# One decoder layer on one core: the first four products run as a group, x turned by VectorE and DRAM past 512 columns, and dense scores as three fp32r products

## The chip, the cores and the metric

The kernel runs on one core of one Trainium2 chip. The metric is the device time of one execution in microseconds (us). The kernel before takes 2049.03 us, the median of three runs that lie between 2048.91 and 2049.04.

## What is computed

One layer over 256 tokens of width 2048 in float32: a SwiGLU half, a mixer, a second SwiGLU half, each with an RMS norm ahead of it and a residual, and a last norm.

```python
def swiglu(x, w_gate, w_up, w_down):
    return (jax.nn.silu(x @ w_gate) * (x @ w_up)) @ w_down
...
    x = x + 0.5 * swiglu(rmsnorm(x, ffn1_norm[i]), ffn1_w_gate[i], ffn1_w_up[i], ffn1_w_down[i])
    x = x + hybrid_mixer(rmsnorm(x, mix_norm[i]), w_in[i], ..., w_att_out[i], w_sg_out[i], w_out[i])
    x = x + 0.5 * swiglu(rmsnorm(x, ffn2_norm[i]), ffn2_w_gate[i], ffn2_w_up[i], ffn2_w_down[i])
return rmsnorm(x, final_norm)
```

The mixer projects the normed x by one matrix into queries, keys, values and the two gating branches. Attention has 12 heads of width 128 in three groups of four: the first group looks back 128 tokens (dense), the second takes every 4th token, the third every 16th.

## The kernel before

**Products.** All weights, 1552 tiles of 128 rows by 512 columns, are read once. A weight tile is split into two fp32r halves: ScalarE copies it to `wh` (L139) and VectorE writes the rest, tile minus `wh`, to `wl` (L140). The activations are split likewise into `hi` and `lo` and stand transposed, with 128 features on the partitions and the 256 tokens along a row. A product with a weight tile is then six matmuls (L149): for each of the two halves of the tokens `hh`, `hl` and `lh`, which are hi by `wh`, hi by `wl` and lo by `wh`. Each has the activations as stationary operand and 512 weight columns as moving operand.

**Steps and units.** A step (one entry of `hus`) is two weight tiles, so 12 matmuls; there are 776 steps. A unit is two steps, 1 MB, and is one load (`load_unit`, L121). The raw buffers hold three units, `wh` and `wl` four steps each (`LA + 1`). After the products of step i the loop issues what is due there (`callbacks`) and then splits step i + 4 (`advance`). The order of a matrix's units is laid out by `lay_out`: one gate, up or down matrix slice of 512 columns after the other, and in a pair the last unit of both comes at the end.

**x at the start.** The first norm's gain is folded into x as it is transposed: TensorE transposes 128 by 128 blocks of x into PSUM (`first_transposes`, L235, two blocks for each k of the 16), ScalarE writes `xhi` (L239) and VectorE `xlo` (L240). These transposes stand between the products of the first six steps (`begin`, `early`, `midway`). The other gains are transposed by one more TensorE instruction (`gains`, L761).

**Turns.** Everywhere else a block of 256 tokens by 512 features is transposed by `turn`: VectorE transposes blocks of 32 by 32 (L191), SP writes the block to DRAM (L175) and three steps later reads it back with the partitions exchanged, in four transfers (L181); after that it is split into hi and lo (L163, L164), for x with the gain first (L264).

**Order of work.** Every engine runs its own list in the order in which the program issues it. All loads, turns and writes stand in SP's one queue.

**Scores.** For each of the four head slots and the two parities of the query, the scores of the dense group are one fp32 matmul with 256 keys (L560), read in token order from keys that are stored by parity, and those of the other groups one fp32 matmul each with 128 keys (L562). A turned q or k is copied by parity, one half by ScalarE (L513), one by VectorE (L514).

Of the kernel before, what the change touches and what calls it, by code (L numbers as in the profile page):

```python
# [41 lines left out]
def layer(ctx: ExitStack, tc: tile.TileContext, a, out):  # L42
# [24 lines left out]

    rows = sb.tile([60, P], F32, name="rows")

# [4 lines left out]

    load_rows(0, ACT)
    half = sb.tile([P, 2], F32, name="half")
    DVE.memset(half, -0.5)
    pad = big.tile([P, 96], F32, name="pad")
    DVE.memset(pad[:, 0:2], 0.0)
    junk = sb.tile([P, NC], BF16, name="junk")  # L80
    DVE.memset(junk, 0.0)
    ident = sb.tile([P, P], F32, name="ident")
# [10 lines left out]
    ss = {}  # L93
    gcols = sb.tile([P, 60], F32, name="gcols")

# [23 lines left out]
    raws, splits = {}, {}  # L119

    def load_unit(i, parts=(0, 4)):  # L121
        g, u, _ = hus[2 * i]
        if i in raws:
            r = raws[i]
        else:
            r = raws[i] = big.tile([P, UK, NC], F32, tag="raw", bufs=RAWB, name=f"raw{i}")
        k0 = g["rows0"] + u * UK * P
        src = g["w"][k0:k0 + UK * P, g["c0"]:g["c0"] + NC].rearrange("(k p) c -> p k c", p=P)
        k = slice(*parts)
        SP.dma_start(r[:, k], src[:, k])  # L130

# [110 lines left out]
    def residual(e, n, c, banks, scale, norm):  # L242
# [29 lines left out]
    def ffn(wg, wu, wd, down_post, pair):  # L272
        halves = ((0, 6), (6, 11))
        for hf, (f0, f1) in enumerate(halves):
# [8 lines left out]
            for f in range(f0, f1):  # L283
# [29 lines left out]

                gemm(wg, f * NC, 0, KD, lhs_x, post_gate, pair and f == 0)
                gemm(wu, f * NC, 0, KD, lhs_x, post_up)
            for c in range(4):
                gemm(wd, c * NC, f0 * NC, 4 * (f1 - f0), lhs_h,
                     lambda e, banks, c=c, hf=hf: down_post(e, c, banks, hf == 1), c == 0)

# [3 lines left out]

    ffn(a["ffn1_w_gate"][0], a["ffn1_w_up"][0], a["ffn1_w_down"][0], down1, False)

# [156 lines left out]
    def post_qk(key, gi):  # L482
        def post(e, banks):
            q = sb.tile([P, NT, NSLOT, HD], F32, tag="tmp", bufs=2, name=f"{key}{gi}")

            if "q" not in mix:
                qkT = big.tile([P, 2, NGRP, 2, NSLOT, P], F32, tag="A", name="qkT")
                mix["q"], mix["k"] = qkT[:, 0], qkT[:, 1]
            dst = mix[key][:, gi].rearrange("p r h (t i c) -> p r (h t) i c", t=NT, i=4)

# [58 lines left out]
    def attention(e):  # L549
        for s in range(NSLOT):  # L550
# [5 lines left out]
            def qk(s=s, got=got):  # L556
                got["b"] = [tp_bank(f"sc{s}_{r}") for r in range(2)]
                for r, b in enumerate(got["b"]):
                    q, k = mix["q"][:, :, r, s], mix["k"]
                    PE.matmul(b[:, 0:S], q[:, 0], k[:, 0, :, s].rearrange("p r c -> p c r"), start=True, stop=True)  # L560
                    for g in (1, 2):
                        PE.matmul(b[:, (g + 1) * P:(g + 2) * P], q[:, g], k[:, g, r, s], start=True, stop=True)  # L562

# [86 lines left out]
    for j in range(3):  # L650
        gemm(w_in, o_s + j * NC, 0, KD, lhs_x, post_gelu("vs", j), j == 0)
    for j in range(3):
# [11 lines left out]
    for c in range(4):  # L664
        gemm(a["w_out"][0], c * NC, 0, KD, lambda: (mix["mhi"], mix["mlo"]),
             lambda e, banks, c=c: residual(e, 2, c, banks, 1.0, True), c == 0)

# [87 lines left out]
    norm_open(0)  # L755
    first_banks[1] = mm_bank("xt1")
    first_banks[2] = mm_bank("xt2")

    def gains():
        b = tp_bank("gc1")  # L760
        PE.transpose(b[:, 0:60], rows, ident[0:60, 0:60])  # L761
        DVE.tensor_copy(gcols[:, 16:60], b[:, 16:60])

    at(20, lambda: [load_rows(i) for i in range(1, 4)])
    at(60, gains)
# [15 lines left out]

    def ready(i, whole=False):
        ks = (2 * i, 2 * i + 1)
        for k in ks:
            first_transposes(k)
        for j, k in enumerate(ks):
            first_evac(k)
            if not whole:
                split(i, slice(j, j + 1))
        if whole:  # L790
            split(i)

    def begin():
        split(0, slice(0, 1))
        for k in (0, 1):
            first_transposes(k)
            first_evac(k)
        split(0, slice(1, 2))
        products(0, jjs=(0,))
        for t in range(NT):  # L800
            product(0, 1, t, "hh")
        for k in (2, 3):
            first_transposes(k)
            first_evac(k)
        for kind in ("lh", "hl"):
            for t in range(NT):
                product(0, 1, t, kind)
        for k in (0, 1):
            split(1, slice(k, k + 1))

    begin()
    early = {2: (3, False), 3: (4, True), 5: (7, True)}
    midway = {1: (2, False), 3: (5, True), 4: (6, True)}
    for i in range(n):
        if i in early:
            ready(*early[i])
        if 0 < i < n - LA - 1:
            if i in midway:
                products(i, jjs=(0,), high_first=i < 3)
                ready(*midway[i])  # L820
                products(i, jjs=(1,), high_first=i < 3)
            else:
                products(i, high_first=i < 3)
# [58 lines left out]
```

## Time and profile before

| | |
|---|---|
| median of 3 runs | 2049.03 us |
| the profiled execution, device time | 2049.03 us |
| its span | 2047.3 us |
| TensorE matmuls (PE) busy | 2037.1 us, 100% |
| VectorE (DVE) busy | 1181.6 us, 58% |
| ScalarE (ACT) busy | 973.9 us, 48% |
| moved by DMA | 469.35 MB, mean 229 GB/s |

The span is the time from the first to the last recorded instruction; 1.73 us of the device time lie outside it. PE is the matmul stream and PEld the loading of the stationary operand, which runs beside it. SPq is SP's queue of transfers. The duration of one matmul in the profile includes its way through the array; what it takes of the stream is the distance to the start of the next one.

### The profile page before, as it was taken

What the parts mean: (1) busy time and instruction counts of PE and PEld (TensorE: products, weight loads), DVE (VectorE), ACT (ScalarE), POOL (GpSimd) and SP (SyncE); (2) the same over time, 40 slices, a digit from 0 to 9 for tenths busy, and PEclk for the clock granted to TensorE, in tenths of its full rate; (3) what the DMA queues carried; (4) which work ended last, traced back from release to release, by engine and by line L of the source; (5) the groups of instructions that cost most, each with busy time, mean ns of one, the idle gap of its engine ahead of it and who ended that gap; (6) DMA issues with size and microseconds to landing.
All of it is one profiled execution on the core that took longest, in us unless ns stands there. A gap on an engine that the chain in (4) does not pass through costs nothing.

```text
span 2047.3 us, 23805 instructions
## 1 busy us (share of the span) xinstructions
PE 2037.1 (100%) x9486; PEld 1781.6 (87%) x9486; DVE 1181.6 (58%) x1192; ACT 973.9 (48%) x1070; POOL 12.4 (1%) x18
## 2 busy tenths in 40 slices
PE   9999999999999999999999999999999999999998
PEld 7888888888888888888888888888888888888887
DVE  5555555555556557665665555565555555555554
ACT  6444444444445555455554444564444444444443
POOL 0000000000000000000000000000000000000000
PEclk9999999999999999999999999999999999999999
DMA  7777876666776866787866666777777666777764
GB/s 271 234 236 226 272 245 216 201 222 224 243 229 220 269 201 201 238 280 257 262 212 224 225 225 207 245 250 235 220 243 226 226 205 205 221 222 242 232 214 144
DMA packets 246775, 469.35 MB, mean 229 GB/s; under 512 B 11084, under 2 KB 38536, under 8 KB 246536
## 3 DMA queue, kind: packets, MB, share of 16 engines
q1 hardware_dynamic: 246344, 467.30, 70.4%
q8 instruction: 74, 1.21, 0.2%
q10 hardware_dynamic: 320, 0.53, 0.1%
q14 instruction: 37, 0.30, 0.0%
HBM read 439.22 MB, written 28.57 MB: 228 GB/s over the span
## 4 chain that ended last, share of the span: by engine, by line
PE 99%; issue 0%; ACT 0%; DVE 0%; POOLq 0%; POOL 0%
PE mm L149 98%; PE sc L560 0%; PE sp L458 0%; PE warm L748 0%; PE pv L600 0%; PE sc L562 0%; PE xt L235 0%; PE pv L596 0%; ACT x L716 0%; ACT xhi L239 0%; PE pv L597 0%; DVE x L701 0%; POOLq L877 0%; POOL rf L708 0%; ACT wh L139 0%
## 5 line engine op out<-in xcount | busy, mean ns | idle before, releaser
L140 DVE TENSOR_TENSOR wl<-raw,wh 128x1024 fp32r<-128x1024 f32 (+1 forms) x780 | 948.1, 1218 | 822.1 <-ACT wh L139 818.0
L139 ACT ACTIVATE wh<-raw 128x1024 fp32r<-128x1024 f32 (+1 forms) x780 | 818.0, 1052 | 1007.6 <-PE mm L149 974.6
L149 PE MATMUL mm<-wh,xhi 128*128 128x512 f32 x2144 | 813.8, 380 | 0.5 <-ACT wh L139 0.4
L149 PE MATMUL mm<-wh,xlo 128*128 128x512 f32 x2144 | 812.5, 379 | 0.0
L149 PE MATMUL mm<-wl,xhi 128*128 128x512 f32 x2144 | 811.8, 379 | 0.0
L149 PEld LDWEIGHTS mm<-wh,xhi 128*128 128x128 f32 x2144 | 405.3, 189 | 58.5 <-ACT wh L139 0.8
L149 PEld LDWEIGHTS mm<-wl,xhi 128*128 128x128 f32 x2144 | 405.4, 189 | 57.2
L149 PEld LDWEIGHTS mm<-wh,xlo 128*128 128x128 f32 x2144 | 405.1, 189 | 57.3
L149 PE MATMUL mm<-wh,hhi 128*128 128x512 f32 x704 | 266.8, 379 | 0.0
L149 PE MATMUL mm<-wl,hhi 128*128 128x512 f32 x704 | 266.8, 379 | 0.0
L149 PE MATMUL mm<-wh,hlo 128*128 128x512 f32 x704 | 266.8, 379 | 0.0
L149 PEld LDWEIGHTS mm<-wh,hhi 128*128 128x128 f32 x704 | 133.1, 189 | 18.9
L149 PEld LDWEIGHTS mm<-wl,hhi 128*128 128x128 f32 x704 | 133.1, 189 | 18.9
L149 PEld LDWEIGHTS mm<-wh,hlo 128*128 128x128 f32 x704 | 133.1, 189 | 18.9
L149 PE MATMUL mm<-wh,uT 128*128 128x512 f32 x192 | 58.0, 379 | 0.0
L149 PE MATMUL mm<-wh,mhi 128*128 128x512 f32 x128 | 48.5, 379 | 0.0
L149 PE MATMUL mm<-wl,mhi 128*128 128x512 f32 x128 | 48.5, 379 | 0.0
L149 PE MATMUL mm<-wh,mlo 128*128 128x512 f32 x128 | 48.5, 379 | 0.0
L149 PEld LDWEIGHTS mm<-wh,uT 128*128 128x128 f32 x192 | 36.3, 189 | 5.1
L149 PE MATMUL mm<-wl,uT 128*128 128x512 f32 x96 | 36.4, 379 | 0.0
L304 DVE SCALAR_TENSOR_TENSOR sg<-mm,rstd,sg 128x512 f32<-128x512 f32 x44 | 30.9, 744 | 0.0
L219 ACT ACTIVATE junk<-x 128x512 bf16<-128x512 f32 x30 | 18.9, 629 | 25.0 <-DVE x L247 18.6
(142 smaller groups left out, 596.9 us busy)
## 6 DMA issues: line engine op xcount, KB each, us to landing
raw<-in_w_in_dram SPq DMA_DIRECT2D x92, 1024.0 KB, 5.1
raw<-in_ffn_w_up_dram SPq DMA_DIRECT2D x88, 1024.0 KB, 5.2
raw<-in_ffn_w_down_dram SPq DMA_DIRECT2D x88, 1024.0 KB, 5.1
raw<-in_ffn_w_gate_dram SPq DMA_DIRECT2D x84, 1024.0 KB, 5.1
raw<-in_w_out_dram SPq DMA_DIRECT2D x16, 1024.0 KB, 5.0
raw<-in_w_sg_out_dram SPq DMA_DIRECT2D x12, 1024.0 KB, 5.8
bmh<-bth SPq DMA_DIRECT2D x22, 512.0 KB, 2.9
sg<-bmh SPq DMA_DIRECT2D x88, 128.0 KB, 5.0
```

Source lines behind the costliest of these rows:

```text
L139: ACT.activation(wh[:, k], r[:, k], AF.Copy)
L140: DVE.tensor_tensor(wl[:, k], r[:, k], wh[:, k].bitcast(F32), op=OP.subtract)
L149: PE.matmul(g["ps"][t], act[:, k, t * P:(t + 1) * P], in_turn(w[:, jj]), start=k == 0 and kind == "hh", stop=k == g["nk"] - 1 and kind == ...
L219: ACT.activation(junk, x[:, t, c * NC:(c + 1) * NC], AF.Square, accum_out=ss[n][:, t, c:c + 1])
L304: DVE.scalar_tensor_tensor(two(sg[:, t]), banks[t], rstd[:, t:t + 1], two(sg[:, t]), op0=OP.mult, op1=OP.mult)
```

## The change

- **Group.** The gate and up products of the first two slices form a group of four (`FIRST`). The bounds 1, 2 and 4 make it run the first step (two k) of all four, then the second of all four, then the third and fourth of all four, then steps five to eight of one after the other. Eight PSUM banks collect them: the second slice takes banks of the other tag. A unit of the group can hold steps of two matrices and is then two loads of 512 KB.
- **x.** Only k = 0 to 3 (512 columns) are transposed by TensorE. The other three blocks of 512 columns go through `turn_x`, the same way that later x blocks take: issued at steps 0, 7 and 8, read back at 1, 10 and 11, scaled and split at 4, 12 and 13. x is loaded in this order: columns 0 to 255, 512 to 1023, 256 to 511, and the last two blocks at steps 3 and 4.
- **Gains.** They are transposed by VectorE and DRAM (at steps 32, 36 and 40) instead of TensorE.
- **Scores.** The turned q and k of the dense group are split into hi and lo, k in token order, and the score is three fp32r matmuls with 256 keys. The tiles of q, k, v and the probabilities get other places in memory.
- The memset of `junk` comes first.

```diff
-    def gemm(w, c0, rows0, nk, lhs, post, pair=False):
-        gemms.append(dict(w=w, c0=c0, rows0=rows0, nk=nk, lhs=lhs, post=post, pair=pair))
+    def gemm(w, c0, rows0, nk, lhs, post, group=(1, ()), bank=None):
+        gemms.append(dict(w=w, c0=c0, rows0=rows0, nk=nk, lhs=lhs, post=post, group=group, bank=bank or mm_bank))
...
-            gs = gemms[i:i + 2] if gemms[i]["pair"] else gemms[i:i + 1]
-            i += len(gs)
-            units = [(g, u) for g in gs for u in range(g["nk"] // UK)]
-            if len(gs) == 2:
-                units.sort(key=lambda q: q[1] == q[0]["nk"] // UK - 1)
-            for g, u in units:
-                hus.extend([(g, u, 0), (g, u, 1)])
+            size, bounds = gemms[i]["group"]
+            steps = [(g, q) for g in gemms[i:i + size] for q in range(g["nk"] // 2)]
+            i += size
+            steps.sort(key=lambda s: sum(s[1] >= (b if b > 0 else s[0]["nk"] // 2 + b) for b in bounds))
+            hus.extend((g, q // 2, q % 2) for g, q in steps)
+    PAIR = (2, (-2,))
+    FIRST = (4, (1, 2, 4))
...
+        (g, u, j), (h, v, _) = hus[2 * i], hus[2 * i + 1]
+        first, last = parts
+        while first < last:
+            end = last if (g, u) == (h, v) or first > 1 else min(last, 2)
+            q, w, k = (g, u, 0) if first < 2 else (h, v, 2)
+            o = 2 * hus[2 * i + k // 2][2] - k if (g, u) != (h, v) else 0
+            k0 = q["rows0"] + w * UK * P
+            src = q["w"][k0:k0 + UK * P, q["c0"]:q["c0"] + NC].rearrange("(k p) c -> p k c", p=P)
+            SP.dma_start(raws[i][:, first:end], src[:, first + o:end + o])
+            first = end
...
-            g["ps"] = [mm_bank(f"mm{i}_{q}") for q in range(NT)]
+            g["ps"] = [g["bank"](f"mm{i}_{q}") for q in range(NT)]
...
-    def turn(i, name, q, put, dst, ev, lag=8):
+    def turn(i, name, q, put, dst, ev, lag=8, read=3):
...
-        at(i + 3, back)
+        at(i + read, back)
...
+        turn_x(e + (6 if c == 1 else 2), n, c, 6)
+    def turn_x(i, n, c, lag, read=3):
         def evac(src):
             for j in range(4):
                 v = src[:, 2 * j:2 * j + 2]
             ks = slice(4 * c, 4 * c + 4)
             split_psum(turned(xT["hi"][:, ks]), turned(xT["lo"][:, ks]), src)
 
-        turn(e + (6 if c == 1 else 2), f"x{n}_{c}", 8, put_tokens(lambda: x[:, :, cs]),
-             lambda: flat(sb.tile([P, NT, NC], F32, tag="gate", bufs=2, name=f"xt{n}_{c}")), evac, 6)
+        turn(i, f"x{n}_{c}", 8, put_tokens(lambda: x[:, :, c * NC:(c + 1) * NC]),
+             lambda: flat(sb.tile([P, NT, NC], F32, tag="gate", bufs=2, name=f"xt{n}_{c}")), evac, lag, read)
...
+                bank = tp_bank if group is FIRST and f == 1 else mm_bank
+                gemm(wg, f * NC, 0, KD, lhs_x, post_gate, group if f == 0 else (1, ()), bank)
+                gemm(wu, f * NC, 0, KD, lhs_x, post_up, bank=bank)
...
+                if gi > 0:
+                    dst = by_parity(mix[key, gi])
+                    ACT.activation(dst[:, 0], v[:, 0], AF.Copy)
+                    DVE.tensor_copy(dst[:, 1], v[:, 1])
+                elif key == "q":
+                    hi, lo = (by_parity(p) for p in mix["q", 0])
+                    for r in range(2):
+                        split_psum(hi[:, r], lo[:, r], v[:, r])
+                else:
+                    split_psum(*(p.rearrange("p (m i b) -> p m i b", i=4, b=32) for p in mix["k", 0]), src)
...
-                    PE.matmul(b[:, 0:S], q[:, 0], k[:, 0, :, s].rearrange("p r c -> p c r"), start=True, stop=True)
+                    q0 = [p[:, (4 * r + s) * P:(4 * r + s + 1) * P] for p in mix["q", 0]]
+                    k0 = [p[:, s * S:(s + 1) * S] for p in mix["k", 0]]
+                    for i, j in ((0, 0), (0, 1), (1, 0)):
+                        PE.matmul(b[:, 0:S], q0[i], k0[j], start=i + j == 0, stop=i == 1)
...
-    load_unit(0, (1, 2))
+    for i, k in ((0, 1), (0, 2), (0, 3), (1, 0), (1, 1)):
+        load_unit(i, (k, k + 1))
+    load_x(NC, 2 * NC)
+    for k in (2, 3):
+        load_unit(1, (k, k + 1))
     load_x(S, NC)
-    load_unit(0, (2, 3))
-    load_unit(0, (3, 4))
-    for c in range(1, 4):
-        load_x(c * NC, (c + 1) * NC)
-        load_unit(c, (0, 2))
-        load_unit(c, (2, 4))
+    load_unit(2)
...
+    for i, fn in ((32, more_rows), (36, rows_out), (40, rows_back)):
...
+    for c, i, lag, read in ((1, 0, 4, 1), (2, 7, 5, 3), (3, 8, 5, 3)):
+        turn_x(i, 0, c, lag, read)
+    for c in (2, 3):
+        at(c + 1, lambda c=c: load_x(c * NC, (c + 1) * NC))
...
+    split(0, slice(0, 1))
+    first_x((0, 1))
+    for i, k in ((0, 1), (1, 0), (1, 1), (2, 0), (2, 1)):
+        split(i, slice(k, k + 1))
+        if i < n - LA - 1:
+            products(i, jjs=(0,), high_first=i < 4)
+            if i == 2:
+                first_x((2, 3))
+            products(i, jjs=(1,), high_first=i < 4)
+        if i != 1:
+            advance(i + LA + (2 if i else 1))
```

Places where the order changes. **ScalarE at the start**, before: `xt0` to `xt3` are transposed x, `wh0` and `wh1` the first two steps' weights.

```order
L139 ACTIVATE wh0_123<-raw0_87 128x512
L239 ACTIVATE xhi0_118<-xt0_127,gcols_84 128x256
L239 ACTIVATE xhi0_118<-xt1_121,gcols_84 128x256
L139 ACTIVATE wh0_123<-raw0_87 128x512
L239 ACTIVATE xhi0_118<-xt2_122,gcols_84 128x256
L239 ACTIVATE xhi0_118<-xt3_152,gcols_84 128x256
L139 ACTIVATE wh1_161<-raw0_87 128x512 x2
L239 ACTIVATE xhi0_118<-xt4_173,gcols_84 128x256
L139 ACTIVATE wh2_181<-raw1_95 128x512
```

and now:

```order
L145 ACTIVATE wh0_118<-raw0_87 128x512
L245 ACTIVATE xhi0_115<-xt0_122,gcols_84 128x256
L245 ACTIVATE xhi0_115<-xt1_125,gcols_84 128x256
L145 ACTIVATE wh0_118<-raw0_87 128x512
L145 ACTIVATE wh1_134<-raw0_87 128x512 x2
L145 ACTIVATE wh2_140<-raw1_93 128x512 x2
L145 ACTIVATE wh3_168<-raw1_93 128x1024
L245 ACTIVATE xhi0_115<-xt2_199,gcols_84 128x256
L245 ACTIVATE xhi0_115<-xt3_202,gcols_84 128x256
L145 ACTIVATE wh4_217<-raw2_100 128x1024
```

The evacuations of the third and fourth transposed blocks stood ahead of the weights of step 1, and stand now behind those of step 3.

**SP's queue**, before, for the loads of steps 8 to 25 (`raw4` to `raw12`):

```order
L130 DMA raw4_315<-in_ffn1_w_up_dram 128x4x512
L130 DMA raw5_317<-in_ffn1_w_up_dram 128x4x512
L130 DMA raw6_319<-in_ffn1_w_up_dram 128x4x512
L130 DMA raw7_341<-in_ffn1_w_up_dram 128x4x512
L130 DMA raw8_380<-in_ffn1_w_gate_dram 128x4x512
L130 DMA raw9_418<-in_ffn1_w_gate_dram 128x4x512
L130 DMA raw10_459<-in_ffn1_w_gate_dram 128x4x512
L130 DMA raw11_495<-in_ffn1_w_gate_dram 128x4x512
L130 DMA raw12_535<-in_ffn1_w_up_dram 128x4x512
```

and now, for steps 12 to 21: `bmx0_2` and `bmx0_3` are the writes of the third and fourth block of x, `xt0_2` and `xt0_3` their reads.

```order
L135 DMA raw6_269<-in_ffn1_w_gate_dram 128x4x512
L135 DMA raw7_303<-in_ffn1_w_up_dram 128x4x512
L181 DMA bmx0_2_324<-btx0_2_321 128x1024
L181 DMA bmx0_3_347<-btx0_3_344 128x1024
L135 DMA raw8_349<-in_ffn1_w_gate_dram 128x4x512
L187 DMA xt0_2_387<-bmx0_2_324 32x4x256 x4
L135 DMA raw9_392<-in_ffn1_w_gate_dram 128x4x512
L187 DMA xt0_3_412<-bmx0_3_347 32x4x256 x4
L135 DMA raw10_444<-in_ffn1_w_up_dram 128x4x512
```

Loads alone before; now two writes and eight reads of x stand between the loads, and the last four behind the load of steps 18 and 19.

**ScalarE at steps 12 to 17**, before:

```order
L139 ACTIVATE wh12_382<-raw6_319 128x1024
L219 ACTIVATE junk_74,ss0_120<-x_81 128x512 x2
L139 ACTIVATE wh13_400<-raw6_319 128x1024
L219 ACTIVATE junk_74,ss0_120<-x_81 128x512 x2
L139 ACTIVATE wh14_420<-raw7_341 128x1024
L219 ACTIVATE junk_74,ss0_120<-x_81 128x512 x2
L139 ACTIVATE wh15_438<-raw7_341 128x1024
L139 ACTIVATE wh16_461<-raw8_380 128x1024
L290 ACTIVATE sg7_359<-mm0_0_138,rstd0_457 128x512
L290 ACTIVATE sg7_359<-mm0_1_139,rstd0_457 128x512
L139 ACTIVATE wh17_479<-raw8_380 128x1024
```

and now:

```order
L145 ACTIVATE wh14_394<-raw7_303 128x1024
L225 ACTIVATE junk_70,ss0_117<-x_81 128x512 x2
L145 ACTIVATE wh15_417<-raw7_303 128x1024
L273 ACTIVATE xt0_2_387<-xt0_2_387,gcols_84 128x2x4x32 x4
L169 ACTIVATE xhi0_115<-xt0_2_387 128x1024
L145 ACTIVATE wh16_446<-raw8_349 128x1024
L273 ACTIVATE xt0_3_412<-xt0_3_412,gcols_84 128x2x4x32 x4
L169 ACTIVATE xhi0_115<-xt0_3_412 128x1024
L145 ACTIVATE wh17_468<-raw8_349 128x1024
L145 ACTIVATE wh18_486<-raw9_392 128x1024
L145 ACTIVATE wh19_502<-raw9_392 128x1024
```

The scaling and splitting of the third block now stands ahead of the weights of step 16, that of the fourth ahead of those of step 17.

## Rows read from the trace of the kernel before

**Rows 1.** The page: busy time of the engines, and one group's weight loads.
```profile
PE 2037.1 (100%) x9486; PEld 1781.6 (87%) x9486; DVE 1181.6 (58%) x1192; ACT 973.9 (48%) x1070; POOL 12.4 (1%) x18
...
L149 PEld LDWEIGHTS mm<-wh,xhi 128*128 128x128 f32 x2144 | 405.3, 189 | 58.5 <-ACT wh L139 0.8
```
**Rows 2.** PE's waits over the span: who, for whom, us, times, longest.
```profile
PE warm L748 <- DVE junk L81: 1.3, 1, 1.3
PE mm L149 <- ACT wh L139: 0.4, 1, 0.4
```
**Rows 3.** The chain in order of time: start us, us, what.
```profile
6.23 2.19 PE mm L149 x8
...
11.65 0.44 PE xt L235 x4
...
22.91 0.44 PE xt L235 x4
23.35 145.04 PE mm L149 x672
168.39 0.20 PE gc L761
...
824.06 2.12 PE sp L458 x18
...
988.88 0.54 PE sc L560 x2
```
**Rows 4.** Stretches: us, busy (count) of PE, PEld, DVE, ACT, POOL, PEclk, DMA, GB/s.
```profile
0.00:5.00 5.00, 3.68 (x9) 1.31 (x10) 0.63 (x5) 2.12 (x3) 0.70 (x6) 1.00 0.55 147
5.00:10.00 5.00, 4.59 (x21) 3.47 (x20) 2.93 (x6) 2.74 (x7) 0.00 (x0) 1.00 0.95 338
10.00:15.00 5.00, 4.91 (x27) 4.34 (x28) 3.91 (x9) 3.65 (x10) 0.00 (x0) 1.00 1.05 399
```
**Rows 5.** Transfers issued in the window 4.9 to 5.3 us: count, KB, us to landing.
```profile
raw<-in_ffn_w_gate_dram SPq DMA_DIRECT2D x1, 512.0 KB, 8.1
```
**Rows 6.** Turns' transfers: count, KB each, median us from issue to landing.
```profile
sg<-bmh SPq DMA_DIRECT2D x88, 128.0 KB, 5.0
...
uroom<-bmu SPq DMA_DIRECT2D x12, 128.0 KB, 7.5
bmq<-btq SPq DMA_DIRECT2D x3, 512.0 KB, 3.1
q<-bmq SPq DMA_DIRECT2D x12, 128.0 KB, 8.5
```
**Rows 7.** Timeline of SP: start, us, queue, line, transfer, count.
```profile
61.36 1.75 SPq L181 DMA_DIRECT2D sg<-bmh  x4
...
860.80 4.67 SPq L181 DMA_DIRECT2D q<-bmq  x4
```
**Rows 8.** A stretch in which four reads of a turn land behind a load.
```profile
64.00:66.00 2.00, 2.00 (x11) 1.76 (x10) 0.64 (x2) 1.06 (x1) 0.00 (x0) 1.00 1.09 257
```
**Rows 9.** Timeline of ACT: start, us, line, operation, count, idle before it.
```profile
51.88 1.06 ACT L139 ACTIVATE wh<-raw 128x1024 fp32r<-128x1024 f32 x1 [1.53 <-PE mm L149]
...
656.71 1.69 ACT L264 ACTIVATE xt<-xt,gcols 128x256 f32<-128x256 f32 x4
658.43 1.06 ACT L163 ACTIVATE xhi<-xt 128x1024 fp32r<-128x1024 f32 x1
...
864.78 2.00 ACT L139 ACTIVATE wh<-raw 128x1024 fp32r<-128x1024 f32 x2 [3.37 <-DMA raw<-in_w_in_dram]
```
**Rows 10.** Timeline of DVE, the same columns.
```profile
52.97 1.23 DVE L140 TENSOR_TENSOR wl<-raw,wh 128x1024 fp32r<-128x1024 f32 x1 [1.36 <-ACT wh L139]
...
876.02 0.44 DVE L514 COPY qkT<-q 128x512 f32<-128x512 f32 x1
876.38 1.29 DVE L191 STREAM_TRANSPOSE btk<-k 128x512 f32<-128x512 f32 x2
877.61 3.45 DVE L140 TENSOR_TENSOR wl<-raw,wh 128x1024 fp32r<-128x1024 f32 x3
```

More of the change, by code (lines that the diff above doesn't have):

```diff
@@ L65, in two @@
         return ap.rearrange("p (a c) -> p a c", a=2)
-    rows = sb.tile([60, P], F32, name="rows")
+    rows = sb.tile([64, P], F32, name="rows")
     def load_rows(i, queue=SP):
@@ L75, in layer @@
     load_rows(0, ACT)
+    junk = sb.tile([P, NC], BF16, name="junk")
+    DVE.memset(junk, 0.0)
     half = sb.tile([P, 2], F32, name="half")
@@ L79, in layer @@
     DVE.memset(pad[:, 0:2], 0.0)
-    junk = sb.tile([P, NC], BF16, name="junk")
-    DVE.memset(junk, 0.0)
     ident = sb.tile([P, P], F32, name="ident")
@@ L93, in layer @@
     ss = {}
[L94 removed]
+    gcols = sb.tile([P, 64], F32, name="gcols")
     gemms = []
@@ L121, in load_unit @@
     def load_unit(i, parts=(0, 4)):
[L122 to L130, printed above, removed]
+        if i not in raws:
+            raws[i] = big.tile([P, UK, NC], F32, tag="raw", bufs=RAWB, name=f"raw{i}")
+        (g, u, j), (h, v, _) = hus[2 * i], hus[2 * i + 1]
[8 more added lines that the diff above has]
+            first = end
     def split(i, k=slice(0, 2)):
@@ L266, in evac, with ffn @@
             split_psum(turned(xT["hi"][:, ks]), turned(xT["lo"][:, ks]), src)
-        turn(e + (6 if c == 1 else 2), f"x{n}_{c}", 8, put_tokens(lambda: x[:, :, cs]),
-             lambda: flat(sb.tile([P, NT, NC], F32, tag="gate", bufs=2, name=f"xt{n}_{c}")), evac, 6)
-    def ffn(wg, wu, wd, down_post, pair):
+        turn(i, f"x{n}_{c}", 8, put_tokens(lambda: x[:, :, c * NC:(c + 1) * NC]),
+             lambda: flat(sb.tile([P, NT, NC], F32, tag="gate", bufs=2, name=f"xt{n}_{c}")), evac, lag, read)
+    def ffn(wg, wu, wd, down_post, group):
         halves = ((0, 6), (6, 11))
@@ L312, in post_up @@
                     turn(e + 2, f"h{e}", 8, put_tokens(lambda: sg), lambda: flat(sg), ev)
-                gemm(wg, f * NC, 0, KD, lhs_x, post_gate, pair and f == 0)
-                gemm(wu, f * NC, 0, KD, lhs_x, post_up)
+                bank = tp_bank if group is FIRST and f == 1 else mm_bank
+                gemm(wg, f * NC, 0, KD, lhs_x, post_gate, group if f == 0 else (1, ()), bank)
+                gemm(wu, f * NC, 0, KD, lhs_x, post_up, bank=bank)
             for c in range(4):
                 gemm(wd, c * NC, f0 * NC, 4 * (f1 - f0), lhs_h,
-                     lambda e, banks, c=c, hf=hf: down_post(e, c, banks, hf == 1), c == 0)
+                     lambda e, banks, c=c, hf=hf: down_post(e, c, banks, hf == 1), PAIR if c == 0 else (1, ()))
     def down1(e, c, banks, last):
         residual(e, 1, c, banks, 0.5, last)
-    ffn(a["ffn1_w_gate"][0], a["ffn1_w_up"][0], a["ffn1_w_down"][0], down1, False)
+    ffn(a["ffn1_w_gate"][0], a["ffn1_w_up"][0], a["ffn1_w_down"][0], down1, FIRST)
     w_in = a["w_in"][0]
@@ L484, in post, with head, by_parity @@
             q = sb.tile([P, NT, NSLOT, HD], F32, tag="tmp", bufs=2, name=f"{key}{gi}")
[L486 to L489, printed above, removed]
+            one = 2 * NSLOT * P
+            if (key, gi) == ("q", 0):
+                parts = big.tile([P, 4, one], F32R, tag="A", name="qk0")
+                mix["q", 0], mix["k", 0] = (parts[:, 0], parts[:, 1]), (parts[:, 2], parts[:, 3])
+            elif (key, gi) == ("q", 1):
+                mix["C"] = big.tile([P, 4, one], F32, tag="C", name="vq")
+                mix["L"] = sb.tile([P, 3, one], F32, tag="L", name="pTk")
+                mix["q", 1], mix["k", 1] = mix["C"][:, 3], mix["L"][:, 2]
+                mix["q", 2] = sb.tile([P, one], F32, tag="W", name="q2")
+                mix["k", 2] = big.tile([P, one], F32, name="k2")
+            def head(nm, g, r, h):
+                return mix[nm, g][:, (4 * r + h) * P:(4 * r + h + 1) * P]
+            mix["head"] = head
+            def by_parity(v):
+                return v.rearrange("p (r m i c) -> p r m i c", r=2, i=4, c=16)
             def rows_of(v):
@@ L558, in qk @@
                 for r, b in enumerate(got["b"]):
-                    q, k = mix["q"][:, :, r, s], mix["k"]
-                    PE.matmul(b[:, 0:S], q[:, 0], k[:, 0, :, s].rearrange("p r c -> p c r"), start=True, stop=True)
+                    q0 = [p[:, (4 * r + s) * P:(4 * r + s + 1) * P] for p in mix["q", 0]]
+                    k0 = [p[:, s * S:(s + 1) * S] for p in mix["k", 0]]
+                    for i, j in ((0, 0), (0, 1), (1, 0)):
+                        PE.matmul(b[:, 0:S], q0[i], k0[j], start=i + j == 0, stop=i == 1)
                     for g in (1, 2):
-                        PE.matmul(b[:, (g + 1) * P:(g + 2) * P], q[:, g], k[:, g, r, s], start=True, stop=True)
+                        PE.matmul(b[:, (g + 1) * P:(g + 2) * P], mix["head"]("q", g, r, s), mix["head"]("k", g, r, s),
+                                  start=True, stop=True)
             def softmax(s=s, got=got):
@@ L650, in layer @@
     for j in range(3):
-        gemm(w_in, o_s + j * NC, 0, KD, lhs_x, post_gelu("vs", j), j == 0)
+        gemm(w_in, o_s + j * NC, 0, KD, lhs_x, post_gelu("vs", j), PAIR if j == 0 else (1, ()))
     for j in range(3):
@@ L665, in layer @@
         gemm(a["w_out"][0], c * NC, 0, KD, lambda: (mix["mhi"], mix["mlo"]),
-             lambda e, banks, c=c: residual(e, 2, c, banks, 1.0, True), c == 0)
+             lambda e, banks, c=c: residual(e, 2, c, banks, 1.0, True), PAIR if c == 0 else (1, ()))
     fin = {}
@@ L755, in layer, with more_rows, rows_out, rows_back @@
     norm_open(0)
[L756 to L765, printed above, removed]
+    def more_rows():
+        POOL.memset(rows[32:64], 0.0)
+        for i in range(1, 4):
+            load_rows(i)
+    def rows_out():
+        d = sb.tile([64, P], F32, name="gd")
+        DVE.transpose(d.rearrange("p (j b) -> p j b", b=32), rows.rearrange("p (j b) -> p j b", b=32))
+        xT["gains"] = m = dram.tile([64, P], F32, name="gm")
+        SP.dma_start(m, d)
+    def rows_back():
+        m = xT["gains"].rearrange("(i a) (j b) -> j a i b", a=32, b=32)
+        for j in range(4):
+            SP.dma_start(gcols[32 * j:32 * j + 32].rearrange("p (i b) -> p i b", i=2), m[j])
+    for i, fn in ((32, more_rows), (36, rows_out), (40, rows_back)):
+        at(i, fn)
     for c in range(4):
@@ L768, in layer @@
     at(12, lambda: norm_rstd(0))
-    loaded, done = 4, 8
+    loaded, done = 3, 3
     def advance(to):
@@ L779, in advance, with first_x @@
             done += 1
-    def ready(i, whole=False):
-        ks = (2 * i, 2 * i + 1)
+    for c, i, lag, read in ((1, 0, 4, 1), (2, 7, 5, 3), (3, 8, 5, 3)):
+        turn_x(i, 0, c, lag, read)
+    for c in (2, 3):
+        at(c + 1, lambda c=c: load_x(c * NC, (c + 1) * NC))
+    def first_x(ks):
         for k in ks:
             first_transposes(k)
-        for j, k in enumerate(ks):
+        for k in ks:
             first_evac(k)
[L788 to L813, printed above, removed]
-    for i in range(n):
[L815 to L823, printed above, removed]
+    split(0, slice(0, 1))
+    first_x((0, 1))
+    for i, k in ((0, 1), (1, 0), (1, 1), (2, 0), (2, 1)):
+        split(i, slice(k, k + 1))
+    for i in range(n):
+        if i < n - LA - 1:
[3 more added lines that the diff above has]
+            products(i, jjs=(1,), high_first=i < 4)
         for f in callbacks.pop(i, []):
             f()
-        if i > 4:
-            advance(i + LA + 2)
+        if i != 1:
+            advance(i + LA + (2 if i else 1))
     for t in range(NT):
```

12 lines of the change are left out of this document (4 added, 8 removed).

## The prediction

> **What bounds the kernel now.** Read first the busy times: PE, the matmul stream, is busy for the whole span, DVE and ACT for about half of it [rows 1]. Then PE's waits: two in all, 1.3 us before the first warm-up matmul and 0.4 us for a weight half at the start [rows 2]. So nothing late bounds the kernel; its own list of matmuls does, at the full granted clock (1.00, the 2.4 GHz level, in the stretches shown [rows 4]). What shortens that list shortens the time, one for one, until something that hides beside it becomes late. The chain in order of time gives the prices: 672 products in 145.04 us, 0.2158 us each, so a step of 12 takes 2.59 us [rows 3].
>
> How much cover is there? In the steady state ACT starts a step's `wh` when PE frees its buffer (idle 1.53 us before, released by PE), and `wl` is done 2.3 us later (51.88 to 54.20) [rows 9, 10]. Its products come three steps, 7.8 us, after the start. A weight half therefore waits 5.5 us for PE. At the very start this lead does not exist yet.
>
> **What the change takes out of PE's list.**
> - Transposes of x: 32 before, 8 left. Six groups of four at 0.44 us, the first and the last of them in [rows 3], are 2.64 us.
> - The transpose of the other gains: 0.20 us [rows 3]. Its way over DVE and SP, eight small transfers around steps 32 to 40, stands beside loads with 5.5 us of lead: nothing. If that lead were gone, a load would be late by their issue, about eight times 0.44 us (a quarter of 1.75 us [rows 7]).
> - Dense scores: eight pairs of fp32 passes at 0.54 us, 4.32 us, become 24 fp32r products with 256 columns. The spatial products have that type and size: 18 in 2.12 us, 0.118 us each [rows 3]. 24 of them are 2.83 us, so 1.49 us go. Bounds: half of a 512-column product, 0.108 us, gives 1.73 us; if each had to wait out its weight load of 0.189 us [rows 1], 4.54 us, a loss of 0.22 us. I take the spatial row, the nearest.
> - Gaps at the start. From 6.23 to 23.35 us are 17.12 us, 60 products (12.95) and 28 transposes at 0.11 (3.08), so 1.09 us are gaps [rows 3]. 0.46 us lie in the first eight products (2.19 us for 8 x 0.2158) and stay, since the first evacuation is the same. The other 0.63 us go: in ACT's list the weights of step 1 stood behind two more evacuations, and now follow step 0's at once.
> In sum 2.64 + 0.20 + 1.49 + 0.63 = 4.96 us.
>
> **What it adds.**
> - The second quarter-block of x (columns 256 to 511) is needed in the middle of step 2, at 6.23 + 0.46 + 30 x 0.2158 = 13.2 us. The same 3 MB are ahead of or in it as were ahead of or in the second half of unit 1 before, which landed at about 4.9 + 8.1 = 13.0 us [rows 5]. Between 0 and 0.6 us (one more 256 KB at 0.4 MB per us [rows 4]); I take 0.2.
> - The split of q and k of the dense group: DVE's copy of 0.44 us becomes two subtractions, together about one split of 1.23 us; 0.8 us more where DVE runs without a gap, and ACT stood idle for 3.37 us behind late loads shortly before [rows 9, 10]. The lead is thin there but not used up: 0, at most 0.8.
> - `junk` first, new places of tiles, two loads for one: no instruction on PE's path, taken as 0.
> - **The turned blocks of x**, the term that decides. Their reads have ACT and DVE waiting in line, and the weights of steps 16 and 17 stand behind them there. Follow the last block. PE comes to step 17 at 6.23 + 0.46 + 0.44 + 0.2 + 17 x 2.59 = 51.4 us.
>  The load of steps 10 and 11 has 8.4 MB up to its end (six units, 1 MB of x, a write, a read). 2.4 MB have moved by 10 us, then 0.40 MB per us [rows 4]: 25.0 us. The read goes at half that rate (257 GB/s at a full DMA share with reads in it [rows 8]), 1.3 us more, and the landing lags by about 1.3 us (an estimate: 3.1 MB had moved at 11.7 us and landed at 13.0): 27.6. Split of step 10: 30.0. DVE then turns block 2, splits step 11, turns block 3: 1.29 + 1.15 + 1.29 [rows 10], 33.7. The write takes 3.1 [rows 6]: 36.8. In the queue follow the load of steps 16 and 17, the four reads of block 2, the load of 18 and 19 and the four reads of block 3: 2.6 us each, 10.4 from about 35.4, plus a tail, 48 to 50 us. A second way to it: the reads of block 3 can be issued from 38 to about 41.5 us, since four took SP 4.67 us in the crowded place and 1.75 in a free one [rows 7], and reads behind a load landed 8.5 us after issue [rows 6]. I take 49.7 for the last.
>  Then ACT scales and copies for 2.65 us (52.4) [rows 9] and only then makes `wh` of step 17 (53.4); DVE subtracts block 3 (53.6) and makes `wl` (54.9). The second product of step 17, due at 51.6, waits for that: 3.3 us, some of it taken already at step 16 by block 2. After it the reads are over and the lead builds up.
>  Bounds: none, if the last reads land 5.0 us after issue, the median of a free turn [rows 6]: 46.3, `wl` at 51.5. From above 10.0 us, this and two loads late by 3.37 us each [rows 9].
> - Block 1, by the same count, is read by about 22.5 us and its step 8 has its `wl` at 27.7, due 28.3: no wait, 0.6 us in hand.
>
> The profiled execution's span is 2047.3 us, with 1.73 us around it: 2049.03, which is the median itself. 2047.3 - 4.96 + 0.2 + 3.3 = 2045.8, and with 1.73 **2047.6 us**.
>
> **A rule against the change.** The transposes cost 0.11 us each on an engine that is never idle [rows 1, 3]. The Trainium skill, VectorE: DVE Perf Modes, Rules for kernel authors, gives a 128 by 128 transpose to TensorE where PSUM will do as the target. By it the 24 should have stayed: 2.64 us of matmul time would be back and the 3.3 us wait gone, 0.7 us better than my sum. For the first block, which has time, the trace speaks the other way.
>
> **The rivals.**
> - *The reads land in time*, as in the free turn. For it: the mean traffic, 15 MB in 50 us, is under the 0.40 MB per us that were moved. Against it: the eight reads stand behind one another and two loads, as those of u and q did (7.5 and 8.5 us [rows 6]). Time: 2047.6 - 3.3 = 2044.3. The Trainium skill, DMA: Bandwidth & Descriptors, Anatomy of one DMA, gives a fixed 2.0 us plus the bytes at 436 GB/s, for the GpSimd path; an estimate by it is 2.3 us for a read of 128 KB, on the side of this rival. The rows show 5.0 to 8.5 us for these reads, so the trace does not agree.
> - *Weights late as well* (the slower side). The place is steps 18 to 21: SP issues their loads behind the reads, and the lead that hid this at 864.78 us, where ACT stood idle for a load for 3.37 us, has not been built up. If both loads are late by that, 6.7 us more: 2054.3. It decides from the point where those loads land 5 us after the last read. Against it: they are issued when step 13's buffer is free, some 10 us ahead.
> - *The scores gain nothing*, each product waiting out its weight load: 1.71 us more, 2049.3. Against it: the spatial products do not.
>
> **How the numbers follow.** My forecast 0.72, reads in time 0.15, weights late 0.05, scores 0.05, something else 0.03. A measurement of this kernel tells about 0.2%, 4.1 us, from no change, so faster is below 2044.9 us: the first rival, save its upper edge, 0.13. Slower is above 2053.1: 0.05. Within: 0.82. The likeliest case's own range is 2045.5 to 2049 (2 us less or 1.4 more wait). For 8 in 10 the range goes from 2044.6, towards the first rival, to 2049.4, the third.
>
> **What would show it.** Right: 8 transposes left at 0.11 us; sums of 0.35 us for three score products; PE without a gap over 0.6 us until 45 us; then two or three waits, together near 3 us, at 48 to 56 us, for ACT's `wh` and DVE's `wl`, with ACT just before them idle for a read of x; none later. Wrong: no such wait (then 2044.3), a wait at step 8, waits for loads after 56 us, or a granted clock below 1.00 behind the wait.

## The result: slower by 0.27%, and the profile after

| | before | after |
|---|---|---|
| median us of ten executions each | 2048.94 | 2055.43 |
| from to | 2048.47 to 2049.06 | 2048.32 to 2057.51 |
| profiled execution, span | 2047.3 | 2054.2 |

The ratio over all executions is 1.0027, 95% interval 1.0018 to 1.0035; the two medians lie 6.49 us, 0.32%, apart. The forecast was 2047.6 with an upper end of 2049.4. The changed kernel also varies by 9 us from one execution to the next, where the kernel before varies by 0.6; one of its ten, 2048.32, lies inside the forecast's range. The profiled execution took 2055.92 us, close to the median.

PE's waits after (columns as in [rows 2]):

```profile
PE mm L155 <- ACT wh L145: 3.1, 2, 2.3
PE mm L155 <- DVE wl L146: 2.6, 3, 1.0
PE warm L781 <- DVE pad L81: 1.3, 1, 1.3
PE mm L155 <- ACT xhi L245: 0.2, 1, 0.2
PE xt L241 <- DMA x<-in_x_dram: 0.2, 1, 0.2
```

These are waits for weight halves, as forecast, and more of them than forecast. The chain in order of time tells what was behind them, and where the rest of the time went (start us, us, what):

```profile
32.27 7.09 DMA bmx<-btx
39.38 6.52 DMA xt<-bmx
45.92 8.45 DMA xt<-bmx
...
54.47 1.72 ACT xt L273 x4
56.21 1.07 ACT xhi L169
...
58.44 1.23 DVE wl L146
59.72 770.97 PE mm L155 x3563
830.68 2.13 PE sp L468 x18
...
884.58 1.33 DVE qk L170 x2
...
997.10 0.36 PE sc L595 x3
```

Read it against [rows 3], at points with the same products behind them:

- Up to the first spatial products: 830.68 against 824.06, 6.62 us later. The transposes of x and of the gains (2.64 + 0.20) are gone from that stretch, so 9.46 us of new time stand in it (6.62 + 2.84).
- From there to the first score: 166.42 us against 164.82 (988.88 - 824.06), 1.60 us more. The chain runs through the split of q there (`qk`, L170, at 884.58).
- From the first score to the end of the span: 1057.1 us against 1058.4, 1.3 us less. Three score products take 0.36 us, two passes took 0.54: eight times 0.18 is 1.44 us.

The sum, 6.62 + 1.60 - 1.3, is the 6.9 us between the spans.

Nearly all of the 9.46 us stands at one place. PE's timeline (start us, us, engine, line, operation, idle before it):

```profile
48.97 0.38 PE L155 MATMUL mm<-wh,xlo 128*128 128x512 f32 x1
51.66 0.48 PE L155 MATMUL mm<-wh,xhi 128*128 128x512 f32 x1 [2.32 <-ACT wh L145]
53.11 0.48 PE L155 MATMUL mm<-wl,xhi 128*128 128x512 f32 x1 [0.96 <-DVE wl L146]
...
58.27 0.48 PE L155 MATMUL mm<-wh,xhi 128*128 128x512 f32 x1 [0.83 <-ACT wh L145]
59.72 0.48 PE L155 MATMUL mm<-wl,xhi 128*128 128x512 f32 x1 [0.97 <-DVE wl L146]
...
61.44 0.63 PE L155 MATMUL mm<-wh,xhi 128*128 128x512 f32 x1
61.87 0.63 PE L155 MATMUL mm<-wl,xhi 128*128 128x512 f32 x1
```

Step 16 is the one from 51.66, step 17 the one from 58.27. PE was free for step 16 at 49.19 (48.97 + 0.22), so without waits the second product of step 17 would have been due at 49.19 + 13 x 0.2158 = 52.0. It ran at 59.72, 7.7 us late. And the last two rows start 0.43 us apart, not 0.22: behind the wait PE ran at half speed. Seven products of step 17 took 0.43 us each and two took 0.34 and 0.30, together 1.7 us more than nine at 0.2158. 7.7 and 1.7 are 9.4. The stretches (columns as in [rows 4]) show the clock:

```profile
50.00:52.00 2.00, 0.34 (x1) 0.19 (x1) 1.30 (x2) 1.61 (x2) 0.00 (x0) 1.00 1.05 218
...
54.00:56.00 2.00, 2.00 (x6) 1.55 (x6) 0.00 (x0) 1.53 (x4) 0.00 (x0) 0.50 0.13 45
...
64.00:66.00 2.00, 2.00 (x11) 1.76 (x10) 0.83 (x1) 1.06 (x1) 0.00 (x0) 1.00 1.05 406
```

From 54 to 56 us the granted clock is 0.50, the 1.2 GHz level, and PE makes 6 products where it makes 11 ten us later; before it fell, PE had stood idle for 3.3 of 4 us (2.32 + 0.96, from 49.19 to 53.11). It fell again behind the second wait. The slow products of step 16 cost nothing of their own, since step 17 waited for the reads anyway.

And why were the reads so late? SP's timeline (start, us, queue, line, transfer) and ACT's:

```profile
29.65 0.37 SPq L135 DMA_DIRECT2D raw<-in_ffn_w_up_dram  x1
32.27 2.67 SPq L181 DMA_DIRECT2D bmx<-btx  x2
35.03 0.51 SPq L135 DMA_DIRECT2D raw<-in_ffn_w_gate_dram  x1
39.38 1.75 SPq L187 DMA_DIRECT2D xt<-bmx  x4
41.22 0.40 SPq L135 DMA_DIRECT2D raw<-in_ffn_w_gate_dram  x1
41.66 4.56 SPq L187 DMA_DIRECT2D xt<-bmx  x4
```
```profile
34.37 1.06 ACT L145 ACTIVATE wh<-raw 128x1024 fp32r<-128x1024 f32 x1 [2.29 <-DMA raw<-in_ffn_w_gate_dram]
...
47.87 1.71 ACT L273 ACTIVATE xt<-xt,gcols 128x256 f32<-128x256 f32 x4 [5.49 <-DMA xt<-bmx]
...
54.47 1.71 ACT L273 ACTIVATE xt<-xt,gcols 128x256 f32<-128x256 f32 x4 [2.86 <-DMA xt<-bmx]
```

The two writes are one row, the second issued at about 34.6. The first write was issued at 32.27 and had landed at 39.38. The load of steps 16 and 17 could still be issued at 35.03, but then SP stood for that landing (3.8 us), ahead of the first read. A 1 MB load had been issued 2.6 us ahead of the write, and the load before that one landed only at 34.3 (ACT's first row). The last read of the last block was issued at 45.92 and landed at 54.37. ACT stood idle for each block, with the weights of steps 16 and 17 behind it in its list.

The kernel before had such a write in its trace. The 3.1 us in [rows 6] are the median of three writes of q. Two of them took 3.1 and 3.0; the first stood behind a load and four reads in the crowd of turns, the place where q and u are turned one after the other. It is the only write among the transfers issued from 853 to 854 us:

```profile
bmq<-btq SPq DMA_DIRECT2D x1, 512.0 KB, 7.7
```

### The profile page after: what moved, and what is told of

The parts are those of the page before. It is cut to its first block, busy times and chain, and to the rows that moved or that the text cites. A ratio compares the mean times of both kernels' runs of the same rounds, so it can differ in the third digit from the quotient of the medians.

```text
span 2054.2 us, 23817 instructions
## 1 busy us (share of the span) xinstructions
PE 2038.1 (99%) x9469; PEld 1780.7 (87%) x9469; DVE 1183.8 (58%) x1189; ACT 977.8 (48%) x1073; POOL 13.2 (1%) x19
## 4 chain that ended last, share of the span: by engine, by line
PE 94%; DMA 3%; DVE 1%; issue 0%; ACT 0%; SPq 0%; POOLq 0%; POOL 0%; ACTq 0%; DVEq 0%
PE mm L155 94%; DMA raw<-in_w_in_dram 1%; DMA xt<-bmx 1%; DMA bmx<-btx 1%; DMA uroom<-bmu 0%; DMA raw<-in_ffn_w_up_dram 0%; DMA x<-in_x_dram 0%; DVE wl L146 0%; PE sp L468 0%; PE pv L634 0%; PE sc L597 0%; ACT wh L145 0%; SPq L135 0%; PE sc L595 0%; DVE btx L197 0%
```

## The experiments

All times are medians beside executions of the kernel before on the same chip (2048.93 to 2048.98 us).

**E1 and E2: each part alone.** E1 has only the scores part of the change, this edit with the split of q and k and the tiles that it needs; E2 has all the rest:

```diff
-                    PE.matmul(b[:, 0:S], q[:, 0], k[:, 0, :, s].rearrange("p r c -> p c r"), start=True, stop=True)
+                    q0 = [p[:, (4 * r + s) * P:(4 * r + s + 1) * P] for p in mix["q", 0]]
+                    k0 = [p[:, s * S:(s + 1) * S] for p in mix["k", 0]]
+                    for i, j in ((0, 0), (0, 1), (1, 0)):
+                        PE.matmul(b[:, 0:S], q0[i], k0[j], start=i + j == 0, stop=i == 1)
```

> Only the change of the dense scores and of q's and k's storage, on the kernel before. Theory (late reads of the turned blocks of x, and the lower clock behind them, cost about 9.4 us; the scores part gives 1.44 us on TensorE, as the rows of the changed kernel show, 0.36 us for three products against 0.54 us for two passes, and the split of q takes about 1.6 us back near 880 us): 2048.95 - 1.44 + 1.6 = 2049.1 us, between 2048.3 and 2049.6, with waits of PE for wl of about 1.3 us in sum where the split of q stands. If those waits were only there because the start had shifted the work: 2047.5 us and no wait. Rival (the loss lies in the scores part): 2053 us or more.

> Only the new start (group of four products, x turned by DVE and DRAM, gains the same way), dense scores as in the kernel before. Theory (late reads): 2.84 us of transposes go, 9.4 us of waits come, 2048.95 - 2.84 + 9.4 = 2055.5 us, with a spread of some us between executions as in the changed kernel, no wait near 880 us. Rival (the loss lies in the scores part): 2046 to 2048 us.

Measured: E1 2047.84 us (2047.18 to 2049.04), ratio 0.9994 (0.9986 to 1.0003). E2 2055.07 us, ratio 1.0027 (1.0017 to 1.0038). The loss is in the start: E2 has it all, as expected (2055.5). For the scores alone the medians lie 1.1 us apart, which the interval does not tell from no change; in the profile three products take 0.36 us and two passes 0.54. In E1's profile PE does not wait at the split of q, against the first expectation and as its second alternative had it; its list of waits has only the two that [rows 2] has:

```profile
PE warm L772 <- DVE junk L81: 1.3, 1, 1.3
PE mm L149 <- ACT wh L139: 0.4, 1, 0.4
```

In E2, where q is not split, the stretch up to the first score is 165.48 us (chain: 992.68 - 827.20), 0.66 more than before; no loss was expected there:

```profile
827.20 2.12 PE sp L468 x18
...
992.68 0.54 PE sc L570 x2
```

So the 1.60 us of the changed kernel are not the price of the split by itself. Whether the split, which stands in the chain there, adds to them behind the new start is not shown.

**E3: no exchange through DRAM for the last two blocks.**

```diff
+        if n == 0 and c > 1:
+            at(i, here)
+            at(i + lag, lambda: evac(got["d"].rearrange("p i m b -> p m i b")))
+            return
```

`here` is VectorE's turn of 32 by 32 blocks, as in `turn`.

> The changed kernel without the two writes to and the eight reads from DRAM of the blocks of x with columns 1024 to 2047: ScalarE takes what DVE has turned in SBUF instead (the exchange between groups of 32 partitions is left out). Everything else stands in its place. Theory (late reads): no wait at steps 16 and 17, clock 1.00 throughout, 2055.4 - 9.4 = 2046.0 us, within 2045 to 2047, and executions agree within 1 us. Rival (the order of the first 32 steps and its loads make the weights late): waits for wh and wl stay behind step 16, 2052 us or more.

Measured: 2046.41 us (2045.47 to 2047.26), ratio 0.9987 (0.9978 to 0.9996). 9.0 us less than the changed kernel, within the expected 2045 to 2047 in the median; the executions spread over 1.8 us, where 1 was expected. In its stretches from 50 to 60 us PE is busy throughout at clock 1.00:

```profile
50.00:55.00 5.00, 5.00 (x25) 4.37 (x24) 3.90 (x4) 1.94 (x3) 0.00 (x0) 1.00 0.71 234
55.00:60.00 5.00, 5.00 (x25) 4.39 (x24) 2.45 (x2) 2.08 (x2) 0.00 (x0) 1.00 0.79 257
```

The order of the group and its loads are not the cause of the loss at the start; the two writes and eight reads are. The loss before the first score is another matter: it stays, 166.58 us (988.15 - 821.57) against 164.82 before.

**E4: the last block later.**

```diff
-    FIRST = (4, (1, 2, 4))
+    FIRST = (4, (1, 2, 4, 6))
...
-    for c, i, lag, read in ((1, 0, 4, 1), (2, 7, 5, 3), (3, 8, 5, 3)):
+    for c, i, lag, read in ((1, 0, 4, 1), (2, 6, 7, 3), (3, 13, 8, 3)):
...
-    for c in (2, 3):
-        at(c + 1, lambda c=c: load_x(c * NC, (c + 1) * NC))
+    for c, i in ((2, 3), (3, 8)):
+        at(i, lambda c=c: load_x(c * NC, (c + 1) * NC))
```

(The squares of the last block follow at step 15, the norm's root at step 16.)

> The changed kernel with the group's steps in one more part, bounds 1, 2, 4, 6, so that columns 1536 to 2047 of x are first needed at step 24 and not at step 18; their load is issued at step 8 (was 4), their turn at step 13 (was 8), their evacuation at step 21 (was 13); columns 1024 to 1535 are turned at step 6 (was 7) and evacuated at step 13 (was 12). Theory (late reads): the four reads left before step 16 have one load and one write less ahead of them, no weights stand behind the last block; a wait of 0 to 3 us at step 16 is left: 2046 to 2049 us. Rival (order of the steps makes the weights late): 2052 us or more.

Measured: 2046.68 us (2044.48 to 2048.41), ratio 0.9989 (0.9980 to 0.9997), as expected. No wait is left at step 16. SP's timeline and ACT's:

```profile
30.66 0.34 SPq L181 DMA_DIRECT2D bmx<-btx  x1
31.11 0.37 SPq L135 DMA_DIRECT2D raw<-in_ffn_w_up_dram  x1
31.53 0.89 SPq L88 DMA_DIRECT2D x<-in_x_dram  x1
...
33.74 1.80 SPq L187 DMA_DIRECT2D xt<-bmx  x4
```
```profile
44.34 1.71 ACT L273 ACTIVATE xt<-xt,gcols 128x256 f32<-128x256 f32 x4 [1.23 <-DMA xt<-bmx]
```

The write now takes 3.1 us (reads issued at 33.74): the load and x's last block, which stood ahead of it, come behind it. Its reads pay part of that back, landing 10.6 us after the first was issued (44.34 - 33.74), where it was 8.5 in the changed kernel (47.87 - 39.38). With the turn 1.6 us earlier, the block is in place 3.5 us earlier. The spatial products start 2.97 us earlier than before (821.09 against 824.06), 2.84 of which are the transposes that are gone, so the finer group costs nothing that shows, and neither does the last block. What is lost in this execution is lost in the crowd of turns of u and q, at a granted clock of 1.00: from the first spatial products to the first score are 168.39 us (989.48 - 821.09), 3.6 more than before.

**E5 and E6: is that crowd a matter of the gains?** Both are E4 with one more edit. E5 transposes the other gains on TensorE as before, E6 makes their scratch area in DRAM longer:

```diff
-    for i, fn in ((32, more_rows), (36, rows_out), (40, rows_back)):
-        at(i, fn)
...
+    at(20, lambda: [load_rows(i) for i in range(1, 4)])
+    at(60, gains)
```
```diff
-        xT["gains"] = m = dram.tile([64, P], F32, name="gm")
+        xT["gains"] = m = dram.tile([P, 4, 256], F32, name="gm").rearrange(...)[0:64 * P].rearrange(...)
```

> E4 with the other gains turned by a TensorE transpose at step 60, as in the kernel before, so that their eight small transfers and the 32 KB scratch area in DRAM (gm) are gone; all later scratch areas of the turns then lie at the same offset within 512 KB as in the kernel before. Open: why PE waits between 840 and 890 us in the changed kernel, in E3 and E4 (1.6, 1.8 and 3.6 us in the profiled executions) and not in E1, which has the split of q too. Theory P (place in DRAM: with gm ahead of them the areas stand 32 KB further on and their reads end later): that wait goes, 2046.7 - 2.5 + 0.2 = 2044.4 us. Theory G (it is the state in which DMA comes to that stretch after the new start, whatever the gains do): 2046.7 + 0.2 = 2046.9 us, waits of 1.5 to 3.5 us stay there.

> E4 with the gains' scratch area in DRAM made 512 KB long (of which 32 KB are used), so that the eight small transfers stay and the later scratch areas of the turns lie at the same offset within 512 KB as in the kernel before. Theory P (place in DRAM): 2046.7 - 2.5 = 2044.2 us, no wait of PE between 840 and 890 us. Theory G (the state of DMA after the new start): as E4, 2046.7 us, waits of 1.5 to 3.5 us there. If E5 loses the wait and this one does not, it is the small transfers themselves.

Measured: 2046.91 us (2045.09 to 2048.60), ratio 0.9989 (0.9980 to 0.9997), and 2046.62 us (2045.81 to 2048.90), ratio 0.9991 (0.9981 to 1.0000). Both as E4, where theory P had 2.3 to 2.5 us less: neither the transfers nor the place explain the wait. E5's profiled execution has no wait in the crowd, E6's loses 0.5 us there: the wait differs from one execution to the next, and a single profile says little of it.

**E7: does the clock cost anything?**

```diff
+        if i in (16, 17):
+            fill(11)
+            product(i, 0, 0, "hh")
+            fill(4)
...
```

`fill` issues matmuls of zeros into the bank that is being summed.

> The changed kernel with 30 more matmuls on TensorE whose two operands are zero (512 columns of bf16, added to a bank that is being summed): 11 ahead of each of steps 16 and 17 and 4 behind the first product of each, where PE waits. Nothing waits for less. Theory (the clock falls because PE stands idle there, and the half-speed products behind the second wait, 8 of them at 0.43 instead of 0.22 us, cost 1.7 us; those behind the first are hidden by the second wait): granted clock 1.00 from 50 to 65 us, 2055.4 - 1.7 = 2053.7 us; where an execution waits less than the 6.5 us of filling, it loses some of that. Rival (the clock is only a sign, time is set by the reads alone): 2055.4 us or more.

Measured: 2052.47 us (2051.03 to 2053.46), ratio 1.0016 (1.0007 to 1.0025), 3.0 us less than the changed kernel, where 1.7 was expected. Its stretches and PE's timeline:

```profile
50.00:55.00 5.00, 4.95 (x24) 2.92 (x23) 2.36 (x2) 2.17 (x4) 0.00 (x0) 1.00 0.75 202
55.00:60.00 5.00, 4.83 (x21) 2.14 (x20) 2.91 (x3) 4.97 (x8) 0.00 (x0) 1.00 0.02 7
```
```profile
55.42 2.55 PE L846 MATMUL mm<-zeros 128*128 128x512 bf16 x11
58.06 0.48 PE L155 MATMUL mm<-wh,xhi 128*128 128x512 f32 x1
58.38 1.04 PE L846 MATMUL mm<-zeros 128*128 128x512 bf16 x4
59.50 0.48 PE L155 MATMUL mm<-wl,xhi 128*128 128x512 f32 x1
...
61.34 0.38 PE L155 MATMUL mm<-wh,xhi 128*128 128x512 f32 x1
61.55 0.38 PE L155 MATMUL mm<-wl,xhi 128*128 128x512 f32 x1
```

Thirty matmuls more make the kernel faster. The second product of step 17 starts at nearly the same time, 59.50 against 59.72, so the reads set it; but the clock stays at 1.00 and the products behind it are 0.22 us apart. At the spatial products this execution is 1.90 us ahead of the changed kernel's (828.78 against 830.68), the 1.7 and 0.2 us of the earlier start. In E2's profiled execution, with the same start, the clock fell behind the first wait only (0.50 from 52 to 54 us, 1.00 from 56 us on), so not every execution pays the 1.7 us. Why the medians lie 3.0 us apart is not settled.

The Trainium skill, TensorE: Matmul & The Clock Gate, HAM oscillation — how this bites in real kernels, tells of a matmul stream that waits for DMA and starts each stretch behind a wait at the lower clock. The changed kernel's trace agrees that the clock is lower behind each of its two waits, 0.50 at 54 to 56 us and 0.58 at 60 to 62; it differs in that the first products behind the second wait, at 59.72 and 60.04, were still 0.32 and 0.21 us ahead of the next.

**E8 and E9: the turns of u further apart.** E8 is E4 with this edit, E9 is E1 with it:

```diff
-            turn(e + 3 + 2 * r, f"u{r}", 8, ...)
+            turn(e + (3, 6, 12)[r], f"u{r}", 8, ...)
```

> E4 with the three turns of u set 3 and 6 steps apart (turns at 3, 6 and 12 steps behind the spatial products, were 3, 5 and 7), so that their writes and reads and those of q and k no longer follow one another within two steps each. E4, E5 and E6 do not differ in time, so neither the gains' transfers nor the place in DRAM make the waits between 840 and 890 us. Theory (DMA is over-full there: in two steps, 5.2 us, a 1 MB load, a 512 KB write and four reads at half rate do not fit at 0.40 MB per us, and weights come late by an amount that varies from one execution to the next): no wait of PE there, 2046.7 - 1.5 = 2045.2 us, and executions closer together. Rival (the varying part is in the start alone): 2046.7 us.

> E1 (only the scores, old start) with the same spreading of u's turns. If the crowd between 840 and 890 us costs E1 its spread (2047.2 to 2049.0 us) above the time without waits (2048.4, the fastest of before, less 1.44): 2047.0 us with executions within 0.5 us of one another. If the spread comes from elsewhere: 2047.8 us as E1.

Measured: E8 2044.88 us, ratio 0.9980 (0.9971 to 0.9989), ten of eleven executions within 2044.41 to 2045.12 and one at 2047.95. E9 2047.56 us (2047.16 to 2049.24), ratio 0.9993 (0.9984 to 1.0002), not told apart from E1: behind the old start the spreading gains nothing that shows, as E9's second alternative had it. In E8's profile PE waits for nothing but the first warm-up matmul, and the stretch from the second spatial products to the first score has no gap (708 products at 0.2158 us):

```profile
833.37 152.81 PE mm L155 x708
986.17 0.36 PE sc L595 x3
```

Its transfers between 830 and 892 us, and those of the changed kernel in the same window (count, KB, median us to landing):

```profile
uroom<-bmu SPq DMA_DIRECT2D x12, 128.0 KB, 5.4
```
```profile
uroom<-bmu SPq DMA_DIRECT2D x12, 128.0 KB, 8.2
```

E8 beats both kernels: 4.05 us less than before, 10.6 less than the change, and 1.8 less than E4, which differs from it in the turns of u alone.

## Why the prediction was wrong

From the forecast's 2047.6 to the 2055.92 of the profiled execution are 8.3 us, nearly all of it in four places: 4.4 of wait at steps 16 and 17 (7.7 where 3.3 were forecast), 1.7 of lower clock behind it, 1.6 before the first score and 0.5 of gaps at the start.

- **Transposes, gains, scores.** Right: 8 transposes are left, and 0.36 us for three score products give 1.44 us, forecast 1.49. The rule against the change did not hold where the blocks have room: E9, which keeps the transposes, takes 2047.56 us, and E8, which turns the blocks, 2044.88.
- **Gaps at the start.** Mis-sized by 0.5 us: from the first product (6.17) to the end of step 15 (49.19) are 192 products (41.43) and 4 transposes (0.44), so 1.15 us of gaps, where 0.46 + 0.2 were forecast. Block 1 made no wait, as forecast.
- **Turned blocks: the place was right, the step that failed is "The write takes 3.1 [rows 6]: 36.8".** The turns by DVE came within 0.9 us of the forecast (last one ended at 34.56, forecast 33.7). But the write was priced at a median of three, two of which stood free, and the reads behind it at their price in a crowd. With a 1 MB load just ahead in the same queue the two writes took 7.1 and 6.0 us. SP issued nothing from 35.5 to the first one's landing at 39.38, and the reads of the last block went out from 41.66 to 46.22 instead of 38 to 41.5. Their 8.45 us to landing were forecast (8.5). So the last landed at 54.4 and not 49.7; from there ACT and DVE took 5.3 us to `wl` of step 17, 59.7, where 5.2 were forecast (54.9). (The 2.65 us for ACT's scaling and copying should be 2.78 by [rows 9]; that is 0.1 us of it.) E3 shows that the loss goes with the writes and reads, E4 the same write at 3.1 us, with the loads behind it. The Trainium skill, DMA: Bandwidth & Descriptors, Queues, rings and completion order, says that SP owns one ring on each of 16 engines, over which a transfer is split, and that each engine consumes descriptors in ring order; the traces agree, 7.1 us behind a load and, in E4, 3.1 us ahead of one.
- **What a wait costs besides itself.** The sum had no term for the clock; it only named a clock below 1.00 among the signs of being wrong. In the profiled execution it is 1.7 us (E7).
- **The split of q and k, "0, at most 0.8".** The split alone costs PE nothing (E1). The 1.60 us lost before the first score stand in the crowd of turns there, and what is lost there differs from profile to profile: 0 in E1, E5 and E8, 0.66 in E2 without the split, 1.76 in E3, 3.6 in E4. That it is the crowd is shown by E8 for E4's start, where the reads of u land in 5.4 us and not 8.9. What makes it worse behind the new start than in the kernel before, and whether the split has a part in it there, is open.
- **The upper end.** The bound of 10.0 us was for weights late as well. The new time, 9.4 us, is nearly that, but by chance and not by that rival: no load was waited for behind step 17. Its chance of 0.05 was given to the wrong mechanism, and the forecast's own range, "2 us less or 1.4 more wait", left no room for reads that go out 4 us later.

## What to carry to other kernels

A round trip through DRAM is priced in the queue in which it stands: add up what was issued ahead of each leg, and do it for all legs alike. Look at the slowest transfer of a kind and where it stood, not only at the median. Put what has a due time ahead of what is only loaded early, or move the due time: here the group's order gave the last block six steps at no cost that shows (E4). And where TensorE waits for several us, price the products that follow at the lower clock as well; here matmuls of zeros in the wait kept the clock up (E7).

## What was not expected of the hardware

- Matmuls whose operands are all zero hold the granted clock at 1.00 through both waits, which in E7 are 3.5 and 3.9 us long, and no cost of them shows beside the wait.
- One and the same transfer in the same order takes a different time from one profile to the next: the first of the two writes 7.09 us in the changed kernel's, 6.74 in E2's and 6.47 in E7's. A kernel without slack for it ranges over 9 us (2048.32 to 2057.51), one with slack over 0.7 (E8, but for one execution in eleven, at 2047.95).
